# A gated FFN's input projection: whole-width split products replaced by seven half-size block products per pair of hidden tiles

## The chip, the cores and the metric

The kernel runs on one core of one Trainium2 chip. The metric is the device time of one launch in microseconds (us). The kernel before takes 932.84 us (median of three runs, 931.05 to 935.1). Engines: PE is TensorE (PEld its weight loads), DVE is VectorE, ACT is ScalarE, POOL is GpSimd, SP is the engine whose queue starts most DMAs.

## What is computed

One decoder layer on x (512 tokens, 1024 channels), float32: a combined input projection with three token mixers (a state-space scan, sparse attention, pooling), a gated merge, an output projection with residual, then the part that the change touches:

```python
h = h + merged @ w_out
hn = _rmsnorm(h, norm2_w)
a_part, b_part = jnp.split(hn @ w_ffn_in, 2, axis=-1)     # 1024 x (2 * 2816)
return h + (jax.nn.silu(a_part) * b_part) @ w_ffn_out      # 2816 x 1024
```

and a final RMSNorm over the channels.

## The kernel before

All matrix products are made in split precision: a float32 operand is split into a high part in the reduced format float32r (a cast on ACT, `ACT.copy(h, src)`) and a low part (`DVE.tensor_tensor(l, src, h, subtract)`). Three matmuls make one product term: high weight by high input, high weight by low input, low weight by high input (`product`, three `PE.matmul` for each 128-row slice k of the contraction).

- **Stages.** Input projection with the mixers; the branch projections; `w_out` (token-major, `token_major`); the norm of its result, tile of 128 tokens by tile (`residual`, `after_out`, which transposes the rows on PE into feature-major `hnh` and `hnl`); the FFN input; the FFN output (`token_major` again); final norm and stores.
- **FFN input.** 11 steps j. Each loads 256 gate columns (`ra`) and 256 value columns (`rb`) of `w_ffn_in`, 1 MB each, on SP's queue, into a ring of two raw buffers. For each of the 22 hidden tiles i of 128 columns it splits two weight slices of 128 x 1024 (tiles `wh`, `wl`, rings of three) and makes two products of 8 slices: 8 x 3 matmuls of 512 moving columns for the gate, as many for the value. They land in two PSUM banks `f`. Then `silu` on ACT, a product on DVE, and the split of the hidden tile into `hidh`, `hidl`.
- **First tiles.** The first three of these products are made in halves of 256 tokens (`for c in halves`), so that they can start before the norm of the last two token tiles is done; their weights (`early`, tiles `eh`, `el`) are split ahead, during `w_out`.
- **Order.** PE's order is the program's order (`manual_schedule`); small streams (norms, transposes) are put between the matmuls by `tick`. On the other engines a scheduler places the instructions when the program is built; each engine then runs its list strictly in order.
- **FFN output.** `token_major` walks the 22 hidden tiles; of each, 24 matmuls of 512 columns with the hidden tile as the weight side, and one split of a 128 x 1024 row block of `w_ffn_out`. The split hidden tiles are there since the stage before.

Of the kernel before, what the change touches and what calls it, by code (L numbers as in the profile page):

```python
# [8 lines left out]
F32 = mybir.dt.float32  # L9
# [4 lines left out]
P = 128  # L14
T = 512
# [80 lines left out]
def kernel(  # L96
# [91 lines left out]
    def nm(s):  # L188
        uid[0] += 1
        return f"{s}_{uid[0]}"  # L190
# [4 lines left out]
    def slot(tag, name, dtype=F32, shape=(P, T)):  # L195
        return spool.tile(list(shape), dtype, name=nm(name), tag=tag, bufs=SLOTS[tag])
# [4 lines left out]
    def pmm(name="mm"):  # L201
        return psum.tile([P, T], F32, name=nm(name), tag="mm")
# [7 lines left out]
    def tsl(t):  # L210
        return slice(t * P, (t + 1) * P)

    def load_cols(parts, nk):
        raw = wpool.tile([P, 2048], F32, name=nm("raw"), tag="raw", bufs=2)
        width = 2048 // nk
        rv = raw.rearrange("p (k n) -> p k n", k=nk)
        o = 0
        for ap, c0, n in parts:
            SP.dma_start(rv[:, :, o:o + n], ap[:, c0:c0 + n].rearrange("(k p) n -> p k n", p=P))
            o += n  # L220
        assert o <= width
        return rv
# [17 lines left out]
    def split(src, h, l):  # L240
        ACT.copy(h, src)
        DVE.tensor_tensor(l, src, h, op=OP.subtract)
# [51 lines left out]
    def to_feature_major(src, hs, ls, t, get):  # L294
        for g in range(2):
            ps = get("tr")
            for i in range(4):
                PE.transpose(ps[:, tsl(i)], src(4 * g + i), ident)
            pv = ps.rearrange("p (k t) -> p k t", k=4)
            split(pv, hs[g][:, :, tsl(t)], ls[g][:, :, tsl(t)])  # L300
            yield "now"
# [652 lines left out]
            st.live[0][1] = at + NLAG  # L954
        return st

    def token_major(w, nk, ah, al, tail, done, ahead=None):
        acc = {}
        for t in range(NT):
            for hf in range(2):  # L960
                acc[t, hf] = pmm("acc") if t < 2 else paux("acc")
        keep = []

        def term(t, k, wh, wl, hfs=(0, 1)):
            a, b = ah(k)[:, tsl(t)], al(k)[:, tsl(t)]
            for hf in hfs:
                cs = slice(hf * T, hf * T + T)
                PE.matmul(acc[t, hf], lhsT=a, rhs=wh[:, cs], start=(k == 0), stop=False)
                PE.matmul(acc[t, hf], lhsT=a, rhs=wl[:, cs], start=False, stop=False)
            for hf in hfs:  # L970
                cs = slice(hf * T, hf * T + T)
                PE.matmul(acc[t, hf], lhsT=b, rhs=wh[:, cs], start=False, stop=(k == nk - 1))
            tick()

        for k in range(nk):
            if k % 2 == 0:
                raw = wpool.tile([P, 2, D], F32, name=nm("raw"), tag="raw", bufs=2)
# [31 lines left out]
    fnrow = load_row(final_norm_w, "fnrow")  # L1009

    hnh = [slot("xn", "hnh", R32, (P, 4, T)) for _ in range(2)]
    hnl = [slot("xn", "hnl", R32, (P, 4, T)) for _ in range(2)]

    def residual(t, a0, a1, row, last):
        st = small([P, 2], "st2")
        ys = []
        for hf, a in ((0, a0), (1, a1)):
            if last and hf == 0:
                with tc.issue_after(stats[0]):
                    DVE.tensor_tensor(xr[t][hf], a, xr[t][hf], op=OP.add)  # L1020
            else:
                DVE.tensor_tensor(xr[t][hf], a, xr[t][hf], op=OP.add)
            ACT.activation(a, xr[t][hf], AF.Square, scale=RD, accum_out=st[:, hf:hf + 1])
            y = slot("m", "rows")
            (DVE if last or (row is fnrow and hf) else POOL).tensor_tensor(y, xr[t][hf], row[hf], op=OP.mult)
            ys.append(y)
        rs = rstd_of(st)
        for hf in range(2):
            if row is fnrow and hf == 1:
# [3 lines left out]
        return ys  # L1033

    def after_out(t, a0, a1):
# [5 lines left out]
    early, fraw = {}, []  # L1041

    def parted(src):
        hs, ls = [], []
        for g in range(2):
            tag = "yP" if len(early) < 2 else "A"
            h, l = slot(tag, "eh", R32), slot(tag, "el", R32)
            hv, lv = h.rearrange("p (k n) -> p k n", k=4), l.rearrange("p (k n) -> p k n", k=4)
            split(src[:, 4 * g:4 * g + 4, :], hv, lv)
            hs.append(hv)  # L1050
            ls.append(lv)
        return lambda k: hs[k // 4][:, k % 4, :], lambda k: ls[k // 4][:, k % 4, :]

    def early_weights():
        ra = load_cols([(wfi, 0, 256)], KD)
        rb = load_cols([(wfi, FH, 256)], KD)
        fraw.extend((ra, rb))
        for key, r in ((("a", 0), ra[:, :, tsl(0)]), (("b", 0), rb[:, :, tsl(0)]), (("a", 1), ra[:, :, tsl(1)])):
            early[key] = parted(r)
# [7 lines left out]
    def hh(k):  # L1067
        return hnh[k // 4][:, k % 4, :]

    def hl(k):  # L1070
        return hnl[k // 4][:, k % 4, :]

    hidh, hidl, hbig = [], [], []
    for j in range(NH // 2):
        if j:
            ra = load_cols([(wfi, 256 * j, 256)], KD)
            rb = load_cols([(wfi, FH + 256 * j, 256)], KD)
        else:
            ra, rb = fraw
            for key in early:  # L1080
                early[key] = (pmm("f"), *early[key])
            for c in halves:
                for ps, wh, wl in early.values():
                    product(ps, wh, wl, hh, hl, KD, c)
                for st in norms2[2:]:
                    need(st)
        for s in range(2):
            i = 2 * j + s
            pab = []
            for key, r in ((("a", i), ra), (("b", i), rb)):  # L1090
                if key in early:
                    pab.append(early[key][0])
                    continue
                wh, wl = split_w(r[:, :, tsl(s)], (P, KD, P))
                ps = pmm("f")
                product(ps, wh, wl, hh, hl, KD)
                pab.append(ps)
            pa, pb = pab
            sa = slot("th", "silu")
            ACT.activation(sa, pa, AF.Silu)  # L1100
            DVE.tensor_tensor(sa, sa, pb, op=OP.mult)
            if 14 <= i < 18:
                if i == 14:
                    hbig = [slot("yA", "hidb", R32, (P, 4, T)) for _ in range(2)]
                h, l = hbig[0][:, i - 14, :], hbig[1][:, i - 14, :]
            else:
                tag = "m" if i < 4 else "yP" if i < 8 else "A" if i < 14 else "T1" if i < 20 else "T2"
                h = slot(tag, "hidh", R32)
                l = slot(tag, "hidl", R32)
            split(sa, h, l)  # L1110
            hidh.append(h)
            hidl.append(l)

    of = out[0]

# [33 lines left out]
```

## Time and profile before

| | |
|---|---|
| median of three runs | 932.84 us |
| the profiled execution | 933.53 us, of which 931.8 us is the span from its first to its last instruction |
| PE, PEld | 906.9 us (97%), 751.2 us (81%) of the span |
| DVE, ACT, POOL | 489.2 us (52%), 359.3 us (39%), 96.4 us (10%) |
| granted TensorE clock | 0.998 |
| HBM | 91 GB/s over the span |

PE's busy time counts overlapping matmuls: a row's duration is longer than the distance to the next one's start. What a matmul costs in a dense run is the distance of two starts. "[3.88 <-PE f]" behind a row means that the engine stood idle for 3.88 us before it and that a PE instruction on f ended this. The scheduler leaves lists in order, so an instruction that waits holds all behind it on its engine.

### The profile page before, as it was taken

To read this page: it belongs to the slowest core of one execution; us is meant where nothing else is said; L and a number is where in the kernel's file an instruction comes from. 1 tells how busy PE (TensorE), PEld (TensorE's weight loads), DVE (VectorE), ACT (ScalarE), POOL (GpSimd) and SP (SyncE) were. 2 spreads that over 40 slices of the span, in tenths; PEclk is the share of its full clock that TensorE was granted. 3 is DMA by queue.
4 is the path that set the end of the run, shared out by engine and by line. 5 is a ranking of instruction groups with operands and counts; after the bars stand their busy time and mean duration, and the time that the engine had idled before them with its cause. 6 is when DMAs were issued, how large, how long until landed. Compare 5 with 4: busy or idle time off the path is not lost.

```text
span 931.8 us, 11002 instructions
## 1 busy us (share of the span) xinstructions
PE 906.9 (97%) x4401; PEld 751.2 (81%) x4401; DVE 489.2 (52%) x792; ACT 359.3 (39%) x618; POOL 96.4 (10%) x96
## 2 busy tenths in 40 slices
PE   6999899999999999999999999999999999999997
PEld 4877678888888877778888889888888888888885
DVE  6487999955654576658343355233333333322226
ACT  5446433355564344545322256222232232212114
POOL 2061000001100133332000021000000000000001
PEclk9999999999999999999999999999999999999999
DMA  7132112232221311215223241222222332332212
GB/s 239 46 113 77 59 46 91 76 106 83 74 70 58 101 46 57 91 57 181 91 92 135 90 136 46 90 91 91 91 91 92 111 114 91 95 117 105 91 46 90
DMA packets 70964, 85.42 MB, mean 92 GB/s; under 512 B 4025, under 2 KB 61953, under 8 KB 70914
## 3 DMA queue, kind: packets, MB, share of 16 engines
q1 hardware_dynamic: 69234, 82.38, 27.3%
q10 hardware_dynamic: 1680, 2.36, 0.8%
q8 instruction: 34, 0.56, 0.2%
q14 instruction: 16, 0.13, 0.0%
HBM read 82.63 MB, written 2.10 MB: 91 GB/s over the span
## 4 chain that ended last, share of the span: by engine, by line
PE 85%; DVE 9%; issue 2%; ACT 2%; POOL 1%; DMA 0%; SPq 0%; POOLq 0%; ACTq 0%; DVEq 0%
PE mm L90 26%; PE f L90 26%; PE acc L90 17%; PE up L90 8%; DVE work L90 2%; DVE wl L90 2%; DVE top L90 2%; PE yatt L90 1%; PE yd L90 1%; PE ptr L90 1%; PE logit L90 1%; POOL win L90 1%; PE yo L90 1%; DVE qT L90 1%; PE state L90 1%
## 5 line engine op out<-in xcount | busy, mean ns | idle before, releaser
L90 DVE TENSOR_TENSOR wl<-raw,wh 128x1024 fp32r<-128x1024 f32 (+1 forms) x150 | 183.5, 1224 | 228.1 <-ACT wh L90 222.8
L90 ACT CAST wh<-raw 128x1024 fp32r<-128x1024 f32 (+1 forms) x152 | 152.7, 1005 | 378.9 <-PE f L90 155.6
L90 PE MATMUL mm<-xnh,wh 128*128 128x512 f32 (+1 forms) x480 | 193.9, 404 | 0.2 <-ACT xnh L90 0.2
L90 PE MATMUL mm<-xnl,wh 128*128 128x512 f32 (+1 forms) x480 | 183.5, 382 | 1.0 <-DVE xnl L90 1.0
L90 PE MATMUL mm<-xnh,wl 128*128 128x512 f32 (+1 forms) x480 | 183.7, 383 | 0.0
L90 PE MATMUL f<-hnh,wh 128*128 128x512 f32 x328 | 127.6, 389 | 0.0
L90 PE MATMUL f<-hnl,wh 128*128 128x512 f32 x328 | 127.6, 389 | 0.0
L90 PE MATMUL f<-hnh,wl 128*128 128x512 f32 x328 | 127.6, 389 | 0.0
L90 PEld LDWEIGHTS mm<-xnh,wl 128*128 128x128 f32 x480 | 91.1, 190 | 17.9
L90 PEld LDWEIGHTS mm<-xnl,wh 128*128 128x128 f32 x480 | 91.5, 191 | 16.1 <-DVE xnl L90 1.5
L90 PEld LDWEIGHTS mm<-xnh,wh 128*128 128x128 f32 x480 | 91.7, 191 | 15.5 <-issue 1.6
L90 PEld LDWEIGHTS f<-hnh,wl 128*128 128x128 f32 x328 | 61.6, 188 | 12.9
L90 PEld LDWEIGHTS f<-hnl,wh 128*128 128x128 f32 x328 | 61.6, 188 | 12.8
L90 PEld LDWEIGHTS f<-hnh,wh 128*128 128x128 f32 x328 | 61.6, 188 | 12.6
L90 DVE TENSOR_TENSOR silu<-silu,f 128x512 f32<-128x512 f32 x22 | 15.1, 688 | 78.2 <-PE f L90 78.2
L90 PE MATMUL acc<-wh,hidh 128*128 128x512 f32 x144 | 56.0, 389 | 0.0
L90 PE MATMUL acc<-wl,hidh 128*128 128x512 f32 x144 | 56.0, 389 | 0.0
L90 PE MATMUL acc<-wh,hidl 128*128 128x512 f32 x144 | 44.8, 389 | 0.0
L90 POOL TENSOR_TENSOR rows<-xr,fnrow 128x512 f32<-128x512 f32 x3 | 3.9, 1292 | 353.1 <-issue 347.5
L90 POOL TENSOR_TENSOR xbc<-xbc,tap 128x509 f32<-128x509 f32 x12 | 14.0, 1164 | 194.8 <-DVE xbc L90 167.1
L90 PEld LDWEIGHTS acc<-wl,hidh 128*128 128x128 f32 x144 | 27.0, 188 | 5.6
L90 PEld LDWEIGHTS acc<-wh,hidl 128*128 128x128 f32 x144 | 27.0, 188 | 5.6
(250 smaller groups left out, 1322.9 us busy)
## 6 DMA issues: line engine op xcount, KB each, us to landing
raw<-in_w_in_dram SPq DMA_DIRECT2D x26, 1024.0 KB, 5.0
raw<-in_w_ffn_in_dram SPq DMA_DIRECT2D x22, 1024.0 KB, 4.9
raw<-in_w_ffn_out_dram SPq DMA_DIRECT2D x11, 1024.0 KB, 5.0
raw<-in_w_up_ssd_dram SPq DMA_DIRECT2D x4, 1024.0 KB, 4.7
raw<-in_w_out_dram SPq DMA_DIRECT2D x4, 1024.0 KB, 5.0
xb<-in_x_dram SPq DMA_DIRECT2D x4, 512.0 KB, 4.3
raw<-in_w_in_dram SPq DMA_DIRECT2D x4, 512.0 KB, 5.9
raw<-in_w_up_pool_dram SPq DMA_DIRECT2D x2, 1024.0 KB, 4.9
```

What stands on the lines that cost most here:

```text
L90: return fn(*args, **kw)
```

## The change

The 512 tokens are cut into two halves of 256 and the 1024 contraction rows into two halves of 512; gate and value columns are taken as the two block rows of one matrix. For each of 11 units u (256 gate and 256 value columns) seven products p replace eight block products. Each has 4 slices of 128, two blocks c of 128 output rows, three matmuls of 256 columns: 24 x 7 = 168 matmuls for a unit, where 96 of 512 columns stood. The input blocks are B11, B21 (first 256 tokens, two channel halves), the differences T1 to T4, and B22. The weight sums and differences are made by DVE on the raw weights, in place (`combine_w`).

Bank r1 of a unit collects products 1, 6, 7 and 4 one after the other. Between them ACT copies its state out (`keep`, into `p1`, `u2`, `u3`), since two results need the state after 1, after 6 and after 7. Products 2 and 5, 3 have banks of their own. DVE adds the copies (`added`), ACT applies silu, DVE multiplies. Split hidden tiles are no longer made in this stage: the hidden tile stays whole (`hid`) and is split in the FFN output (`hidden_part`). The residual rows are written to a DRAM scratch and read back for the FFN output. The first three units begin with their products 1 and 2; then come 5, 6, 7, 4, 3. All others run 1, 5, 6, 2, 7, 4, 3. Weights of the product at place n + 2 are split when place n is issued (`prepare`).

```diff
 def after_out(t, a0, a1):
     hn = residual(t, a0, a1, n2row, False)
-    yield
-    yield from to_feature_major(lambda k: hn[k // 4][:, tsl(k % 4)], hnh, hnl, t, pmm if t < 2 else paux)
+    for hf in range(2):
+        SP.dma_start(hrows[t][hf], xr[t][hf])
+    yield
+    for g in range(2):
+        ...
+        if t < 2:
+            split(pv, tl[:, 0, :, cs], tl[:, 1, :, cs])
+        for j in range(2):
+            ACT.copy(w[j][:, :, cs], pv[:, 2 * j:2 * j + 2, :])
+        yield "now"
+def combine_x(name):
+    ...
+    for j in range(2):
+        if x is not None:
+            DVE.tensor_tensor(o[j], x[j], y[j], op=OP.subtract)
+        split(o[j], h[j], l[j])
+def combine_w(u, p):
+    if p == 5:
+        for j in range(2):
+            DVE.tensor_tensor(first_sum[u][j], raws[u][1][:, 2 * j:2 * j + 2, :], raws[u][1][:, 4 + 2 * j:6 + 2 * j, :], op=OP.add)
+    elif p == 6:
+        DVE.tensor_tensor(quarter(u, 1, 0), quarter(u, 0, 0), quarter(u, 1, 0), op=sub)
+        for j in range(2):
+            a = raws[u][0][:, 2 * j:2 * j + 2, :]
+            DVE.tensor_tensor(a, first_sum[u][j], a, op=sub)
+    elif p == 3:
+        DVE.tensor_tensor(quarter(u, 0, 1), quarter(u, 0, 1), quarter(u, 0, 0), op=sub)
+def weights(u, p):
+    h = wpool.tile([P, 4, HW], R32, name=nm("wh"), tag="wh")
+    l = wpool.tile([P, 4, HW], R32, name=nm("wl"), tag="wl")
+    ...
+def early_weights():
+    ...
+    for u in range(2):
+        for p in (1, 2):
+            h, l = (pieces("A" if p == 1 else "yP", "early", R32) for _ in range(2))
+            for j in range(2):
+                split(quarter(u, *WHERE[p])[:, 2 * j:2 * j + 2, :], h[j], l[j])
+def multiply(u, p):
+    r, first = {1: (1, True), 6: (1, False), 7: (1, False), 4: (1, False), 2: (2, True), 5: (3, True), 3: (3, False)}[p]
+    ...
+    for c in range(2):
+        o = ps[:, c * HW:c * HW + HW]
+        for k in range(4):
+            a, b = xh[k // 2][:, k % 2, :], xl[k // 2][:, k % 2, :]
+            PE.matmul(o, lhsT=wh(k)[:, tsl(c)], rhs=a, ...)
+            PE.matmul(o, lhsT=wh(k)[:, tsl(c)], rhs=b, ...)
+            PE.matmul(o, lhsT=wl(k)[:, tsl(c)], rhs=a, ...)
+            tick()
+def keep(u, name):
+    snap[u, name] = slot("th", name)
+    ACT.copy(snap[u, name], res[u, 1])
+def added(u, r, name):
+    c = slot("A", "cs")
+    DVE.tensor_tensor(c, res[u, r], snap[u, name], op=OP.add)
+    return c
+def collect(u, p):
+    if p == 1:
+        keep(u, "p1")
+    elif p == 2:
+        a0 = added(u, 2, "p1")          # then silu of two halves on ACT
+    elif p == 6:
+        keep(u, "u2")
+    elif p == 7:
+        keep(u, "u3")
+        gate_[u] = added(u, 3, "u3")
+    elif p == 4:
+        ...                              # hid (first tokens) *= r1
+    elif p == 3:
+        a1 = added(u, 3, "u2")          # silu, then hid (last tokens) = a1 * gate_
+plan = [(u, p) for u in range(LEADERS) for p in (1, 2)]
+for u in range(NU):
+    plan += [(u, p) for p in ((5, 6, 7, 4, 3) if u < LEADERS else (1, 5, 6, 2, 7, 4, 3))]
+for n, (u, p) in enumerate(plan):
+    ...
+    if n in XSUMS:
+        combine_x(XSUMS[n])
+    prepare(n + 2)
+    multiply(u, p)
+    collect(u, p)
-token_major(w_ffn_out[0], NH, lambda k: hidh[k], lambda k: hidl[k], 3, after_ffn)
+token_major(w_ffn_out[0], NH, lambda k: hidden_part(k, 0), lambda k: hidden_part(k, 1), 3, after_ffn, tag="xn")
```

**Where the lists change.** ACT, one unit from the fourth on (here the sixth; `raw_5625` holds its value weights, `raw_5623` its gate weights, `raw_5857` the gate weights of the next unit; `r_1063` is its bank r1). Products in PE's order: 2 (`wh_5992`), 7 (`wh_6021`), 4 (`wh_6051`), 3 (`wh_6087`), then the next unit's 1 (`wh_6123`) and 5 (`wh_6157`).

```order
L90 CAST wh_6051<-raw_5625 128x1024
L90 COPY u_1070_6049<-r_1063_5965 128x512
L90 CAST wh_6087<-raw_5623 128x1024
L90 ACTIVATE hid_6083<-cs_6081 128x256
L90 ACTIVATE hid_6085<-cs_6081 128x256
L90 CAST wh_6123<-raw_5857 128x1024
L90 COPY u_1081_6119<-r_1063_5965 128x512
L90 CAST wh_6157<-S_1085_6127 128x512
L90 CAST wh_6157<-S_1086_6128 128x512
L90 CAST wh_6195<-raw_5857 128x1024
```

The same place before:

```order
L90 CAST wh_5704<-raw_5700 128x1024
L90 CAST hidh_5631<-silu_5628 128x512
L90 CAST wh_5733<-raw_5702 128x1024
L90 ACTIVATE silu_5693<-f_5639 128x512
L90 CAST wh_5769<-raw_5700 128x1024
```

What moved: where ACT had casts and one silu on a bank that nothing adds to any more, it now has three copies of a bank that PE goes on adding to. The copy after product 7 (`u_1081`) stands behind the cast of the next unit's first weights (`wh_6123`), whose ring place product 7 itself gives back.

ACT in the first three units (here the first: products 7 `wh_4974`, 4 `wh_5013`, 3 `wh_5049`, then product 5 of the second unit, `wh_5089`):

```order
L90 CAST wh_5013<-raw_4490 128x1024
L90 CAST T_945_5004<-whole_4639 128x512
L90 CAST wh_5049<-raw_4488 128x1024
L90 COPY u_950_5042<-r_895_4714 128x512
L90 CAST wh_5089<-S_956_5057 128x512
L90 COPY u_958_5085<-r_895_4714 128x512
L90 CAST wh_5089<-S_957_5058 128x512
L90 CAST wh_5124<-raw_4492 128x1024
```

What moved: product 7 now follows product 6 at once on the same bank, so two copies stand between successive products, each behind the cast of a later product's weights: a cast of 128x1024 before `u_950`, one of 128x512 before `u_958`.

ACT at the start of the FFN output (`wh_7370`, `wh_7402`, `wh_7436` are the first three row blocks of `w_ffn_out`, `cs_7335` the last silu of the last unit, `hidh_7374` the high part of hidden tile 0):

```order
L90 CAST wh_7370<-raw_7368 128x1024
L90 COPY u_1222_7281<-r_1210_7162 128x512
L90 CAST wh_7402<-raw_7368 128x1024
L90 CAST wh_7436<-raw_7434 128x1024
L90 ACTIVATE cs_7335<-cs_7335 128x512
L90 CAST hidh_7374<-hid_4800 128x512
L90 CAST hidh_7406<-hid_4802 128x512
```

What moved: the splits of the hidden tiles, which stood in the stage before, now begin behind the last unit's silu.

## Rows read from the trace of the kernel before

**Rows 1.** The page: busy time of the engines, and the shares of the chain of work that ended last, by engine.

```profile
PE 906.9 (97%) x4401; PEld 751.2 (81%) x4401; DVE 489.2 (52%) x792; ACT 359.3 (39%) x618; POOL 96.4 (10%) x96
PE 85%; DVE 9%; issue 2%; ACT 2%; POOL 1%; DMA 0%; SPq 0%; POOLq 0%; ACTq 0%; DVEq 0%
```

**Rows 2.** Busy time by stretch: the stages before `w_out`, and the FFN input. Columns: PE, PEld, DVE, ACT, POOL busy, granted clock, DMA share, GB/s.

```profile
0.00:518.00 518.00, 499.50 (x2522) 411.13 (x2523) 342.68 (x621) 232.19 (x436) 81.83 (x85) 1.00 0.29 90
563.20:805.50 242.30, 242.30 (x1145) 203.75 (x1144) 84.94 (x93) 73.80 (x99) 2.09 (x2) 1.00 0.29 94
```

**Rows 3.** The tile `f` (results of the FFN input): duration of one in ns (least, median, most), first and last start in us. One of the three kinds of 512-column matmuls (all three have 328), then one of the three kinds of 256-column ones of the early halves (48 each), with its weight load.

```profile
L90 PE MATMUL f<-hnh,wh x328: 389/389/396, 582.4 to 804.8; 128*128 128x512 f32 x164
L90 PEld LDWEIGHTS f<-hnh,eh x48: 187/192/192, 563.0 to 582.0; 128*128 128x128 f32 x48
L90 PE MATMUL f<-hnh,eh x48: 278/283/368, 563.2 to 582.1; 128*128 128x256 f32 x48
```

**Rows 4.** Timeline of PE around the last undisturbed run of 256-column matmuls: its first, and the last of it with the first 512-column one. 57 of them lie between 575.61 and 582.44.

```profile
575.61 0.28 PE L90 MATMUL f<-hnh,eh 128*128 128x256 f32 x1
...
582.32 0.28 PE L90 MATMUL f<-hnh,el 128*128 128x256 f32 x1
582.44 0.40 PE L90 MATMUL f<-hnh,wh 128*128 128x512 f32 x1
```

**Rows 5.** Timeline of ACT in the FFN input: a weight cast and the instruction behind it, twice.

```profile
642.32 1.06 ACT L90 CAST wh<-raw 128x1024 fp32r<-128x1024 f32 x1 [3.88 <-PE f L90]
643.30 0.62 ACT L90 CAST hidh<-silu 128x512 fp32r<-128x512 f32 x1
647.76 1.05 ACT L90 CAST wh<-raw 128x1024 fp32r<-128x1024 f32 x1 [3.84 <-PE f L90]
648.72 0.58 ACT L90 ACTIVATE silu<-f 128x512 f32<-128x512 f32 x1
```

**Rows 6.** Timelines of PE and DVE at a border of two products: the last matmul of one that reads its `wh` (one more, on `wl`, stands behind it), and the first of the next; and DVE behind it.

```profile
641.85 0.39 PE L90 MATMUL f<-hnl,wh 128*128 128x512 f32 x1
...
642.31 0.39 PE L90 MATMUL f<-hnh,wh 128*128 128x512 f32 x1
...
642.58 0.69 DVE L90 TENSOR_TENSOR silu<-silu,f 128x512 f32<-128x512 f32 x1 [3.38 <-PE f L90]
643.41 1.23 DVE L90 TENSOR_TENSOR wl<-raw,wh 128x1024 fp32r<-128x1024 f32 x1
644.56 0.68 DVE L90 TENSOR_TENSOR hidl<-silu,hidh 128x512 fp32r<-128x512 f32 x1
```

**Rows 7.** Timelines of ACT and PE in the first stage, where PE waits for ACT: the releasing instruction, the two matmuls behind the wait, the next one.

```profile
80.54 0.60 ACT L90 ACTIVATE relu<-score 128x512 f32<-128x512 f32 x1
81.19 0.74 PE L90 MATMUL score<-ki,qi 128*128 128x512 f32 x2 [0.40 <-ACT relu L90]
81.77 0.40 PE L90 MATMUL mm<-xnh,wh 128*128 128x512 f32 x1
```

**Rows 8.** Groups of DVE and of ACT between 563.2 and 805.6 us: count, busy us, mean ns of one, idle before.

```profile
L90 DVE TENSOR_TENSOR wl<-raw,wh 128x1024 fp32r<-128x1024 f32 x43 | 53.7, 1249 | 77.6 <-ACT wh L90 76.1
L90 DVE TENSOR_TENSOR silu<-silu,f 128x512 f32<-128x512 f32 x21 | 14.4, 688 | 74.9 <-PE f L90 74.9
L90 ACT CAST wh<-raw 128x1024 fp32r<-128x1024 f32 x44 | 46.3, 1052 | 161.1 <-PE f L90 155.6 <-issue 3.9 <-DMA raw<-in_w_ffn_in_dram 1.6
```

**Rows 9.** Loads of `w_ffn_in`: the page's row of DMA issues (count, KB, median us from issue to landing), and one pair on SP's queue.

```profile
raw<-in_w_ffn_in_dram SPq DMA_DIRECT2D x22, 1024.0 KB, 4.9
655.55 5.80 SPq L219 DMA_DIRECT2D raw<-in_w_ffn_in_dram  x2
```

**Rows 10.** Timelines in `w_out` and behind it: ACT and DVE splitting the early weights, the last weight block of `w_out`, PE where it needs this; then DVE beside a POOL multiplication, the last norm rows on ACT, and the chain's transposes of the last token tile.

```profile
541.57 2.19 ACT L90 CAST eh<-raw 128x512 fp32r<-128x512 f32 x4 [0.72 <-DMA raw<-in_w_ffn_in_dram]
545.23 1.05 ACT L90 CAST wh<-raw 128x1024 fp32r<-128x1024 f32 x1 [1.48 <-PE acc L90]
542.23 2.50 DVE L90 TENSOR_TENSOR el<-raw,eh 128x512 fp32r<-128x512 f32 x4
546.32 1.22 DVE L90 TENSOR_TENSOR wl<-raw,wh 128x1024 fp32r<-128x1024 f32 x1 [1.60 <-ACT wh L90]
547.98 0.39 PE L90 MATMUL acc<-wl,mgh 128*128 128x512 f32 x1
...
565.10 2.25 DVE L90 TENSOR_TENSOR wl<-raw,wh 128x1024 fp32r<-128x1024 f32 x1 [0.27 <-ACT wh L90]
564.97 1.30 POOL L90 TENSOR_TENSOR rows<-xr,n2row 128x512 f32<-128x512 f32 x1 [0.98 <-DVE xr L90]
567.65 0.20 ACT L90 ACTIVATE rs<-ms 128x1 f32<-128x1 f32 x1 [1.02 <-DVE ms L90]
568.23 1.33 ACT L90 ACTIVATE rows<-rows,rs 128x512 f32<-128x512 f32 x2
569.67 0.44 PE tr L90 x4
```

**Rows 11.** Timelines of PE and ACT where the FFN output begins.

```profile
805.28 0.39 PE L90 MATMUL f<-hnh,wl 128*128 128x512 f32 x1
805.51 0.39 PE L90 MATMUL acc<-wh,hidh 128*128 128x512 f32 x1
...
805.52 1.06 ACT L90 CAST wh<-raw 128x1024 fp32r<-128x1024 f32 x1 [3.88 <-issue]
```

More of the change, by code (lines that the diff above doesn't have):

```diff
@@ L976, in token_major @@
             if k % 2 == 0:
-                raw = wpool.tile([P, 2, D], F32, name=nm("raw"), tag="raw", bufs=2)
+                raw = (slot(tag, "raw", F32, (P, 2, D)) if tag else
+                       wpool.tile([P, 2, D], F32, name=nm("raw"), tag="raw", bufs=2))
                 SP.dma_start(raw, w[k * P:(k + 2) * P, :].rearrange("(k p) n -> p k n", p=P))
@@ L1024, in residual @@
             y = slot("m", "rows")
-            (DVE if last or (row is fnrow and hf) else POOL).tensor_tensor(y, xr[t][hf], row[hf], op=OP.mult)
+            (DVE if last or (row is not n2row and hf) else POOL).tensor_tensor(y, xr[t][hf], row[hf], op=OP.mult)
             ys.append(y)
@@ L1028, in residual @@
         for hf in range(2):
-            if row is fnrow and hf == 1:
+            if row is not n2row and hf == 1:
                 DVE.tensor_scalar(ys[hf], ys[hf], rs, None, OP.mult)
@@ L1033, in residual, with k4, pieces @@
         return ys
+    dram = ctx.enter_context(tc.tile_pool(name="rows", bufs=1, space=bass.MemoryType.DRAM))
+    hrows = [[dram.tile([P, T], F32, name=f"hrows_{t}_{hf}", tag=f"hrows_{t}_{hf}") for hf in range(2)] for t in range(NT)]
+    HW = T // 2
+    NU = NH // 2
+    G = dict(skip_group_check=True)
+    def k4(ap):
+        return ap.rearrange("p (k t) -> p k t", k=4)
+    def pieces(tag, name, dtype=F32):
+        return [slot(tag, name, dtype, (P, 2, HW)) for _ in range(2)]
+    blocks, whole = {}, {}
@@ L1035, in after_out, with block @@
+    def block(name):
+        if name not in blocks:
+            if name in ("B11", "B21", "T1", "B22"):
+                tl = slot("xn" if name in ("B11", "B21") else "yA", name, R32, (P, 2, 4, HW))
+                blocks[name] = [[tl[:, i, 2 * j:2 * j + 2, :] for j in range(2)] for i in range(2)]
+                blocks[name].append(tl)
+            else:
+                blocks[name] = [pieces("xbc", name, R32) for _ in range(2)]
+        return blocks[name]
     def after_out(t, a0, a1):
@@ L1054, in early_weights @@
-    def early_weights():
[L1055 to L1059, printed above, removed]
+        cs = tsl(t % 2)
+        for g in range(2):
+            ps = (pmm if t < 2 else paux)("tr")
+            for i in range(4):
+                PE.transpose(ps[:, tsl(i)], hn[g][:, tsl(i)], ident)
+            pv = k4(ps)
+            if t < 2:
+                tl = block(("B11", "B21")[g])[2]
+                split(pv, tl[:, 0, :, cs], tl[:, 1, :, cs])
+            w = whole.setdefault((g, t // 2), [])
+            if not w:
+                w.extend(pieces("A" if t < 2 else "T2", "whole"))
+            for j in range(2):
+                ACT.copy(w[j][:, :, cs], pv[:, 2 * j:2 * j + 2, :])
+            yield "now"
@@ new lines, in combine_x @@
+    def combine_x(name):
+        b11, b21, b12, b22 = (whole[g, t] for t in range(2) for g in range(2))
+        o, x, y = {"T1": (b11, b12, b11), "T2": (b11, b22, b11), "T3": (b12, b22, b12), "T4": (b21, b21, b11),
+                   "B22": (b22, None, None)}[name]
+        h, l = block(name)[:2]
+        for j in range(2):
+            if x is not None:
+                DVE.tensor_tensor(o[j], x[j], y[j], op=OP.subtract)
+            split(o[j], h[j], l[j])
+    wfi = w_ffn_in[0]
+    raws, ahead_raw, first_sum, parts, res, snap = {}, {}, {}, {}, {}, {}
@@ new lines, with load_raw, load_unit, quarter @@
+    gate_, hid = {}, {}
+    def load_raw(u, ab, tag):
+        rv = (wpool.tile([P, KD, 256], F32, name=nm("raw"), tag="raw", bufs=2) if tag == "raw"
+              else slot(tag, "raw", F32, (P, KD, 256)))
+        c0 = ab * FH + 256 * u
+        SP.dma_start(rv, wfi[:, c0:c0 + 256].rearrange("(k p) n -> p k n", p=P))
+        return rv
+    def load_unit(u):
+        if 2 <= u < NU:
+            raws[u] = [load_raw(u, ab, "xn" if u % 2 else "raw") for ab in range(2)]
+    def quarter(u, i, j):
+        return raws[u][i][:, 4 * j:4 * j + 4, :]
@@ new lines @@
+    WHERE = {1: (0, 0), 2: (0, 1), 3: (0, 1), 4: (1, 1), 6: (0, 0), 7: (1, 0)}
+    RHS = {1: "B11", 2: "B21", 3: "B22", 4: "T4", 5: "T1", 6: "T2", 7: "T3"}
+    def weights(u, p):
+        if (u, p) in parts:
+            return
+        h = wpool.tile([P, 4, HW], R32, name=nm("wh"), tag="wh")
+        l = wpool.tile([P, 4, HW], R32, name=nm("wl"), tag="wl")
+        if p == 5:
+            for j in range(2):
+                split(first_sum[u][j], h[:, 2 * j:2 * j + 2, :], l[:, 2 * j:2 * j + 2, :])
+        elif u in ahead_raw and p in (1, 2):
+            i, j = WHERE[p]
+            split(ahead_raw[u][:, 4 * j:4 * j + 4, :], h, l)
+        else:
+            split(quarter(u, *WHERE[p]), h, l)
+        parts[u, p] = (lambda k: h[:, k, :]), (lambda k: l[:, k, :])
@@ new lines, in multiply @@
+    def multiply(u, p):
+        r, first = {1: (1, True), 6: (1, False), 7: (1, False), 4: (1, False), 2: (2, True), 5: (3, True), 3: (3, False)}[p]
+        if first:
+            res[u, r] = (pmm if r == 1 else paux)(f"r{r}")
+        ps = res[u, r]
+        wh, wl = parts.pop((u, p))
+        xh, xl = block(RHS[p])[:2]
+        for c in range(2):
+            o = ps[:, c * HW:c * HW + HW]
+            for k in range(4):
+                a, b = xh[k // 2][:, k % 2, :], xl[k // 2][:, k % 2, :]
+                PE.matmul(o, lhsT=wh(k)[:, tsl(c)], rhs=a, start=first and k == 0 and c == 0, stop=False, **G)
+                PE.matmul(o, lhsT=wh(k)[:, tsl(c)], rhs=b, start=False, stop=False, **G)
+                PE.matmul(o, lhsT=wl(k)[:, tsl(c)], rhs=a, start=False, stop=k == 3 and c == 1, **G)
+                tick()
@@ new lines, in keep @@
+    def keep(u, name):
[10 more added lines that the diff above has]
+            a0 = added(u, 2, "p1")
+            for c in range(2):
+                i = 2 * u + c
+                hid[i] = slot("T2" if i < 4 or 8 <= i < 12 else "T1" if i < 8 else "yP" if i < 20 else "A", "hid")
+                ACT.activation(hid[i][:, :HW], a0[:, c * HW:c * HW + HW], AF.Silu)
+        elif p == 6:
[4 more added lines that the diff above has]
+        elif p == 4:
+            for c in range(2):
+                h = hid[2 * u + c][:, :HW]
+                DVE.tensor_tensor(h, h, res[u, 1][:, c * HW:c * HW + HW], op=OP.mult)
+        elif p == 3:
+            a1 = added(u, 3, "u2")
+            ACT.activation(a1, a1, AF.Silu)
+            for c in range(2):
+                cs = slice(c * HW, c * HW + HW)
+                DVE.tensor_tensor(hid[2 * u + c][:, HW:], a1[:, cs], gate_[u][:, cs], op=OP.mult)
@@ L1065 @@
         need(st)
[L1067 to L1112, printed above, removed]
@@ new lines @@
+    prepare(0)
+    prepare(1)
+    for n, (u, p) in enumerate(plan):
+        if n == 3:
+            for st in norms2[2:]:
+                need(st)
+        if n in XSUMS:
[3 more added lines that the diff above has]
+        collect(u, p)
+    fnrow = load_row(final_norm_w, "fnrow")
+    xr = [[slot("xbc", "xr") for _ in range(2)] for _ in range(NT)]
+    for t in range(NT):
+        for hf in range(2):
+            SP.dma_start(xr[t][hf], hrows[t][hf])
+    hidden = {}
@@ L1114, with hidden_part @@
+    def hidden_part(k, part):
+        if k not in hidden:
+            h, l = slot("A", "hidh", R32), slot("A", "hidl", R32)
+            split(hid[k], h, l)
+            hidden[k] = h, l
+        return hidden[k][part]
     of = out[0]
```

36 lines of the change are left out of this document (21 added, 15 removed).

## The prediction, made before the changed kernel ran

> **What bounds the kernel now.** I read the page's busy times and its chain first: PE is busy 97% of the span and makes 85% of the chain [rows 1]. That alone says little about one stage, so the busy times by stretch come next: between 563.2 and 805.5 us PE is busy for all of 242.3 us, DVE for 84.9, ACT for 73.8 [rows 2]. The FFN input is matmuls back to back, and what it costs is their number times their distance.
>
> The distances come from starts, not from durations. From 582.44 [rows 4] to 805.51 [rows 11] stand 3 x 328 = 984 matmuls of 512 columns [rows 3]: 223.07 / 984 = 226.7 ns each, although a row lasts 389. The early halves show the other size: 57 matmuls of 256 columns between 575.61 and 582.44 [rows 4], 6.83 / 57 = 119.8 ns. Half the columns cost 53% of the time.
>
> **The matmuls: -18.9 us.** Before: 984 x 226.7 ns + 3 x 48 x 119.8 ns = 223.1 + 17.2 = 240.3 us. After: 11 units x 168 x 119.8 ns = 221.4 us. An eighth of the products goes, and 6% of a matmul comes back each time it is cut in half; 7.9% of the stage is left. The transposes of the norm stay as they are.
>
> A weight load lasts 192 ns [rows 3], longer than the distance of 120, and is hidden. The Trainium skill (TensorE: Matmul & The Clock Gate, Measured speedup vs the span model) says that a weight load overlaps running matmuls only where it uses another row group, which no load here does; by that rule each of the 1,848 matmuls would lie open, and the sum would be the last rival's. The trace does not agree.
>
> **The copies out of r1: +25.1 us.** Product 7 adds to the bank that ACT must have copied as it stood after product 6, and product 4 to the one as it stood after 7. In units from the fourth on, product 2 (24 x 0.12 = 2.9 us) lies between 6 and 7, and product 5 between 1 and 6; these two copies are covered: cast, copy and latencies take 1.85 us as worked out below. Nothing lies between 7 and 4. There ACT's list has the cast for the next unit's product 1 ahead of the copy, and that cast waits for product 7 too, because the ring of three gives it product 7's place. I count from the slot in which PE would start product 4:
> - The last matmul of product 7 that reads `wh` starts two slots earlier and lasts 0.28 [rows 3]; in the same situation ACT started 0.08 behind the end of such a matmul: 641.85 + 0.39 [rows 6] against 642.32 [rows 5]. So the cast starts at -0.24 + 0.28 + 0.08 = 0.12.
> - A cast of 128 x 1024 holds ACT for 0.97 (642.32 to 643.30, 647.76 to 648.72 [rows 5]): 1.09.
> - The copy of a 128 x 512 bank takes the 0.58 of the silu on such a bank [rows 5]: 1.67.
> - PE starts 0.05 behind ACT (80.54 + 0.60 to 81.19), and its first matmul behind a wait takes 0.13 longer than two distances leave (81.77 - 81.19 - 2 x 0.227) [rows 7]: **1.85 us**.
>
> Eight units pay this once. The first three have 6, 7, 4 in direct succession. Each pays 1.85 at product 7; at product 4 the first two pay 1.43, since the cast in front has 512 columns there (0.55, [rows 10]), the third 1.85. Together 12 x 1.85 + 2 x 1.43 = 25.1 us. Bounds: 1.00 for each of the 14, were the copy first in line (the product's last matmul ends 0.16 into the slot, 0.08, then 0.58 and 0.18), and 2.2 if ACT's two instructions take their whole row durations (1.05, 0.59) and the latencies double. I take the value from ACT's own rows, because nothing else is in that list.
>
> **DVE, hidden.** A unit needs eight instructions of 1024 columns at 1.15 (643.41 to 644.56 [rows 6]), nine of 512 at 0.61 (2.50 less an overlap of 0.07, over four [rows 10]) and four of 256, between 0.3 and 0.61: 9.2 + 5.5 + 1.5 = 16.2 us; with whole row durations (1.25, 0.69 [rows 8]) 18. PE's unit is 168 x 0.1198 + 1.85 = 22.0. A ring place comes free three products ahead of its next use; cast and low part take 2.3 us of the two products left, 5.8, so DVE may be late by some 3 us. The cover is PE's time alone; there are 4 us of it in a unit. ACT needs ten of 22. Loads: two of 1 MB per unit in 5.8 us [rows 9]; they start when the unit two before has split its product 3 and are wanted by DVE some 7 us later. DVE would wait for them with its other work behind it, which its 3 us cover.
>
> **The start: +1.6 us.** (a) The early weights grow from six to eight splits of 512 columns, all ahead of `w_out`'s last weight block in the lists. ACT casts from 541.57 at 0.55 each [rows 10], so until 545.97; then the block's cast to 546.94, its low part on DVE to 548.15. PE wants it at 547.98 [rows 10]: 0.2 us, and 0.2 for the restart. (b) The rows of the last token tile reach PE just in time now (568.23 + 1.33 against 569.67 [rows 10]), about 6.4 us into the stage; the new place of their transposes is as deep. ACT gets eight more copies of 256 columns ahead of them (0.32 to 0.55 each, no row has this shape; I take the low end, since a shorter copy cannot be dearer), 2.6 us; 0.4 comes back since a copy of 0.58 stands where a cast of 0.97 stood, and 1.0 is idle there today [rows 10]. That leaves 1.2. Bounds of the start 0 to 5, the upper one if DVE's instructions beside POOL's take 2.25 in place of 1.25, as one did [rows 10, 8]. The x differences follow under the second rival.
>
> **The end of the stage: +2.9 us.** Today the FFN output follows without a gap (805.28, 805.51 [rows 11]), since its hidden tiles lie ready. Now the first one's split stands in ACT's list behind a cast that waits for the last product's ring place and behind the last silu: 0.12 + 0.97 + 0.55 + 0.60 (the split's cast) + 0.18 = 2.4 us until the first matmul. Its low part comes 0.5 us later than the fifth matmul wants it (DVE: low part of a weight block, two 256-column products, then this). Bounds 1 and 4. Later hidden tiles are hidden: 1.1 + 0.6 us of ACT and 1.25 + 0.69 of DVE in 24 x 0.227 = 5.4 us of PE. Residual rows to DRAM and back: hidden, the reload is wanted a hundred us later.
>
> **The sum.** -18.9 + 25.1 + 1.6 + 2.9 = +10.7 us. Against the profiled execution's own 933.53 us that is 944.2; the median of the runs shown lies 0.7 lower, so I give **944**. With the waits a quarter us shorter or longer (14 x 0.25 = 3.5) and the bounds of start and end: 938 to 951. A measurement of this kernel tells about 0.5% (4.7 us) from no change.
>
> **Rivals.**
> - **Only the copy is paid, not slower** (7%). If the cast in front of each copy found its ring place free before product 7 ends, the 14 waits would shrink to about 1.00: -18.9 + 14.0 + 4.5 = -0.4 us, 933. Below (18.9 - 4.5) / 14 = 1.03 us a wait the change is no slower; below 0.7 it would be faster by over 0.5%. [...]
> - **DVE late in the first units** (11%). From product 1 of the first unit to its product 3 DVE has some 8 instructions of 1024 and 29 of 512 columns (norm, weight sums, T1 to T4, B22): 27 us, with whole row durations and 0.1 of waiting at each 34, in eleven products and two waits of PE, 34.9. Past that point PE pays. With a fifth more than the 34, from waits on ACT's splits and on POOL as in [rows 10], it pays 6: 950.
> - **Late loads** (2%). At twice the 5.8 us [rows 9] the loads miss DVE by 4 us and PE by 1 to 2 in each unit: 960. Loads at a third of the DMA time [rows 2] speak against it.
> - **Weight loads come into the open** (2%). With 192 ns per matmul in place of 120 the stage grows by 1,848 x 0.072 = 133 us: 1,077. Against it: the 57 matmuls [rows 4] are the same shape on the same kind of operands. Nor does the clock look endangered: it is 1.00 in the first stretch, where PE idles for 18 us in all [rows 2].
>
> That the products are made as said is plain from the list: 1,848 matmuls of 256 columns on the banks r1 to r3.
>
> **Chances.** Forecast 78%, rivals 7, 11, 2, 2. Faster by over 0.5%: 2 (what of the first rival lies below 0.7 us a wait). Within: 9 (the rest of it, and the forecast's lowest end). Slower: 89. The range takes the forecast's bounds and most of the second rival: 937 to 953.
>
> **What would show it.** In the changed profile: r matmuls at 120 ns; in each unit from the fourth one idle time of PE of 1.7 to 1.9 us that ends with ACT's copy, with a cast of 1024 columns right before that copy; six such waits in the first three units; 22 us a unit; a gap of 2 to 3 us where the FFN output begins; DVE busy for 16 to 18 us a unit. It is wrong if PE waits for DVE's low parts instead, if the copies find the bank in time, or if 256-column matmuls stand wider apart than 125 ns, where this term alone grows by 10 us.

## The result: 1.3% slower, and the profile after

The changed kernel takes 945.67 us (median of 4 runs, 943.78 to 945.93) against 933.16 for the kernel before in the same comparison: a ratio of 1.013, 95% interval 1.0104 to 1.0156. The prediction was 944, slower, from 937 to 953. The profiled execution took 945.64 us, its span 943.9, which is 12.1 more than the 931.8 before.

The page of the changed kernel, the two rows that answer to [rows 1]:

```profile
PE 896.4 (95%) x5121; PEld 774.6 (82%) x5121; DVE 612.4 (65%) x972; ACT 419.9 (44%) x729; POOL 95.6 (10%) x96
...
PE 29%; ACT 2%; issue 2%; DVE 1%
```

The waits of PE from 500 us on (what it waited for: us in total, times, longest):

```profile
PE r L90 <- ACT u L90: 20.8, 14, 1.6
PE acc L90 <- ACT hidh L90: 2.1, 1, 2.1
PE acc L90 <- DVE wl L90: 0.3, 1, 0.3
PE tr L90 <- ACT rows L90: 0.3, 1, 0.3
PE acc L90 <- DVE hidl L90: 0.3, 1, 0.3
```

PE is busy for 10.5 us less than before and the kernel is longer all the same: 14 waits for a copy `u` out of r1 have come in, the number the prediction counted. (The chain reaches back over a third of the span here, so its shares can't be set beside those of before.) DVE's busy time has grown by 123 us, and from 500 us on PE waits for it for no more than 0.3 us at any place. By stage: `w_out`, the FFN input (as the second row of [rows 2]) and what follows it (columns as in [rows 2]):

```profile
517.00:564.90 47.90, 47.56 (x217) 39.03 (x216) 23.99 (x34) 22.86 (x46) 8.65 (x7) 1.00 0.36 126
564.90:813.30 248.40, 227.27 (x1865) 224.19 (x1863) 191.28 (x248) 121.24 (x183) 1.88 (x2) 1.00 0.33 110
813.30:940.00 126.70, 121.92 (x530) 100.07 (x528) 53.60 (x70) 42.76 (x68) 3.89 (x3) 0.99 0.20 71
```

The stages begin at their first matmuls and end one matmul slot behind their last: before at 517.83, 563.24 and 805.51, with the end of the span at 931.83; now at 518.83, 564.91 and 813.31, with the end at 943.93. The FFN input takes 248.4 us for 242.3 (+6.1). `w_out` takes 46.1 for 45.4 (+0.7), what follows the FFN input 130.6 for 126.3 (+4.3), and `w_out` begins 1.0 us later, ahead of everything the change touches. Together 12.1.

In the steady units the chain of waits repeats every 21.965 us (start, us, what), and the timelines of PE and ACT at the same place show a wait from inside, as [rows 5, 7] show its parts before:

```profile
652.13 1.04 ACT wh L90
653.17 0.49 ACT u L90
...
653.71 18.87 PE r L90 x156
...
675.68 18.87 PE r L90 x156
```

```profile
652.13 1.04 ACT L90 CAST wh<-raw 128x1024 fp32r<-128x1024 f32 x1 [1.21 <-issue]
653.08 0.58 ACT L90 COPY u<-r 128x512 f32<-128x512 f32 x1
...
651.89 0.28 PE L90 MATMUL r<-T,wl 128*128 128x256 f32 x1
653.71 0.51 PE L90 MATMUL r<-T,wh 128*128 128x256 f32 x2 [1.55 <-ACT u L90]
```

Product 7's last matmul starts at 651.89, the next would follow at 652.01. ACT starts its cast at 652.13, the copy at 653.08, and PE goes on at 653.71. The profile names no releaser for that cast ("issue"); that it waits for product 7 is read from the time, since the last matmul that reads `wh` starts at 651.77 and its row ends at 652.05, 0.08 before the cast, the distance foreseen. The idle time in brackets (1.55) is shorter than the loss, because it counts from the end of a row of 0.28 us and not from the slot 0.12 behind its start, and leaves out the slower restart. The loss is read from starts: 21.965 - 168 x 0.1198 = 1.84 us a unit.

### The profile page after: what moved, and what is told of

It reads as the page before. It is cut to its first block, busy times and chain, and to the rows that moved or that the text cites. A ratio compares the mean times of both kernels' runs of the same rounds, so it can differ in the third digit from the quotient of the medians.

```text
span 943.9 us, 12826 instructions
## 1 busy us (share of the span) xinstructions
PE 896.4 (95%) x5121; PEld 774.6 (82%) x5121; DVE 612.4 (65%) x972; ACT 419.9 (44%) x729; POOL 95.6 (10%) x96
## 5 line engine op out<-in xcount | busy, mean ns | idle before, releaser
L90 DVE TENSOR_TENSOR wl<-raw,wh 128x1024 fp32r<-128x1024 f32 (+1 forms) x171 | 207.6, 1214 | 122.7 <-ACT wh L90 118.3
L90 PE MATMUL r<-T,wh 128*128 128x256 f32 x704 | 129.5, 285 | 20.8 <-ACT u L90 20.8
L90 PEld LDWEIGHTS r<-T,wh 128*128 128x128 f32 x704 | 109.5, 192 | 23.6 <-ACT u L90 23.6
L90 PEld LDWEIGHTS mm<-xnl,wh 128*128 128x128 f32 x480 | 92.2, 192 | 16.2 <-DVE xnl L90 1.6
L90 PE MATMUL r<-T,wl 128*128 128x256 f32 x352 | 99.5, 283 | 0.0
L90 PE MATMUL r<-B,wh 128*128 128x256 f32 x464 | 84.4, 283 | 0.0
L90 PEld LDWEIGHTS r<-B,wh 128*128 128x128 f32 x464 | 72.4, 192 | 0.0
L90 PEld LDWEIGHTS r<-T,wl 128*128 128x128 f32 x352 | 67.5, 192 | 0.0
L90 PE MATMUL r<-B,wl 128*128 128x256 f32 x232 | 65.7, 283 | 0.0
L90 PEld LDWEIGHTS r<-B,wl 128*128 128x128 f32 x232 | 44.5, 192 | 0.0
L90 PEld LDWEIGHTS acc<-wh,hidh 128*128 128x128 f32 x176 | 33.4, 190 | 9.3 <-ACT hidh L90 2.3
```

Of the source, the lines that this page charges most:

```text
L90: return fn(*args, **kw)
```

## Where the FFN output begins

Timelines of PE, ACT and DVE there, which answer to [rows 11], and the granted clock (column 6 behind the stretch, after the five engines) in stretches of 2 us:

```profile
813.19 0.28 PE L90 MATMUL r<-B,wl 128*128 128x256 f32 x1
815.53 0.50 PE L90 MATMUL acc<-wh,hidh 128*128 128x512 f32 x1 [2.06 <-ACT hidh L90]
817.02 1.22 PE L90 MATMUL acc<-wh,hidl 128*128 128x512 f32 x2 [0.30 <-DVE hidl L90]
818.04 0.63 PE L90 MATMUL acc<-wh,hidh 128*128 128x512 f32 x1
...
820.45 0.40 PE L90 MATMUL acc<-wh,hidh 128*128 128x512 f32 x1
...
813.39 1.04 ACT L90 CAST wh<-raw 128x1024 fp32r<-128x1024 f32 x1 [1.78 <-PE r L90]
814.34 0.63 ACT L90 ACTIVATE cs<-cs 128x512 f32<-128x512 f32 x1
814.88 2.69 ACT L90 CAST hidh<-hid 128x512 fp32r<-128x512 f32 x5
...
816.28 3.09 DVE L90 TENSOR_TENSOR hidl<-hid,hidh 128x512 fp32r<-128x512 f32 x5
```

```profile
814.00:816.00 2.00, 0.47 (x2) 0.43 (x3) 1.73 (x4) 2.00 (x5) 0.00 (x0) 1.00 0.83 260
816.00:818.00 2.00, 1.70 (x6) 1.07 (x5) 2.00 (x5) 1.56 (x3) 0.00 (x0) 0.71 0.61 250
818.00:820.00 2.00, 2.00 (x6) 1.57 (x5) 1.38 (x3) 0.00 (x0) 0.00 (x0) 0.50 0.00 0
```

The gap is there with its parts in the order foreseen: cast, silu, the first split, and a second short wait for the low part. What was not foreseen stands behind it. From 817.0 to 820.4 the matmuls lie 0.43 us apart in place of 0.23, at a granted clock that falls to 0.50, the lower of the two levels.

## The experiments

The theory: the block products lose because PE waits for ACT's copy of r1 wherever no other product lies between two that add into r1, and ACT has a weight cast ahead of that copy. The rivals: only the copy matters; VectorE's sums set the pace; halving the matmuls costs more than the rows said. The kernel before was measured again beside the runs, at 933.41 us beside the first four and 933.81 beside the last three, for 933.16 beside the changed kernel; so a difference from the changed kernel's 945.67 is good to about 0.7 us. Where it matters, the stages of the profiled executions are compared as well.

**Another product between 7 and 4, in the later units.**

```diff
-        plan += [(u, p) for p in (... (1, 5, 6, 2, 7, 4, 3))]
...
+            if u == LEADERS:
+                plan.append((u, 1))
+            plan += [(u, 5), (u, 6), (u, 2), (u, 7)] + [(u + 1, 1)] * (u + 1 < NU) + [(u, 4), (u, 3)]
```

> From the fourth unit on, the next unit's product 1 is multiplied between this unit's products 7 and 4, with nothing else changed. Theory (TensorE waits at product 4 for ScalarE's copy of r1, behind a cast of 1024): 2.9 us of matmuls now stand between the end of product 7 and product 4, the cast and the copy take 1.6, so the waits of units 3 to 10 go: 8 x 1.85 = 14.8 us less than the changed kernel's 945.7, about 931; the unit falls from 21.97 us to 20.1, and six waits are left in the first three units. Rival 'only the copy is paid': 8 x 1.00 = 8.0 less, about 937.7. Rival 'VectorE is the bound in the units': the period stays near 22 us, about 945.

Measured: 932.22 us (ratio to the kernel before 0.9985, 0.9976 to 0.9995), 13.5 less than the changed kernel. The waits of PE from 560 us on, and then the chain of waits from 650 to 760 us:

```profile
PE r L90 <- ACT u L90: 10.0, 7, 1.6
```

```profile
649.92 110.16 PE r L90 x918
```

In the steady units PE never stops: 110.16 / 918 = 120.0 ns a matmul. Seven waits are left, one more than expected: the last unit has no next product 1 to put between, so seven waits went, not eight, 7 x 1.84 = 12.9 us, and the FFN input takes 235.8 us, 12.6 less than in the changed kernel. My count was off by one; the price of a wait was not. Neither rival holds here: at 1.00 a wait 7 us would have come, and VectorE, with 16.6 us of work a unit, keeps up with units of 20.1.

**The copy ahead of the cast.**

```diff
-        ACT.copy(snap[u, name], res[u, 1])
+        last_keep[0] = ACT.copy(snap[u, name], res[u, 1]).ins
...
-        weights(u, p)
...
+            with tc.issue_after(last_keep[0]):
+                weights(u, p)
```

> TensorE's order is untouched; on ScalarE the weight casts stand behind the copy of r1 that they stood ahead of. Theory: the copy then starts at the end of the product, and each of the 14 waits falls to about 1.00 us, so 12 x 0.85 + 2 x 0.43 = 11.1 us less than the changed kernel, about 934.6, the unit 21.1 us. Rival 'the cast costs nothing, it is the accumulator's turnaround': nothing moves, about 945.7. If the later casts make the weights late, part of the gain returns as waits for wh or wl.

Measured: 935.2 us (1.0015, 1.0005 to 1.0025), 10.5 less than the changed kernel. The waits of PE from 560 us on, and then the timelines of ACT and PE at product 4 of a steady unit, and at product 4 of the last unit:

```profile
PE r L90 <- ACT u L90: 10.3, 14, 1.5
```

```profile
668.16 0.59 ACT L90 COPY u<-r 128x512 f32<-128x512 f32 x1 [1.28 <-PE r L90]
668.64 1.05 ACT L90 CAST wh<-raw 128x1024 fp32r<-128x1024 f32 x1
...
668.80 0.51 PE L90 MATMUL r<-T,wh 128*128 128x256 f32 x2 [0.68 <-ACT u L90]
```

```profile
794.65 1.04 ACT L90 CAST wh<-raw 128x1024 fp32r<-128x1024 f32 x1 [1.21 <-issue]
795.60 0.58 ACT L90 COPY u<-r 128x512 f32<-128x512 f32 x1
...
796.23 0.51 PE L90 MATMUL r<-T,wh 128*128 128x256 f32 x2 [1.55 <-ACT u L90]
```

All 14 waits are still there. Thirteen have fallen to 0.68 us of idle time, 0.97 by starts (the steady unit takes 21.09 us), where 1.00 was foreseen. The last unit's wait at product 4 has not moved: the cast ahead of its copy makes the first weights of `w_ffn_out`, which the edit doesn't reach, and it still takes 1.55. One wait that keeps its cast keeps its length, thirteen that lose it shrink. PE's order is untouched, so the cast ahead of the copy is shown to cost about 10 of the 25 us (the FFN input falls from 248.4 to 238.4 us, though the transposes of the last token tile come 0.5 later), and the rival by which the cast costs nothing falls. Putting the copy first is the first rival's world, and its 933 is near.

**The kernel before in halves.**

```diff
-                product(ps, wh, wl, hh, hl, KD)
+                for c in halves:
+                    product(ps, wh, wl, hh, hl, KD, c)
```

> The kernel before, with the FFN input's products multiplied in two halves of 256 tokens: 2112 matmuls of 256 columns for 984 of 512 and 144 of 256. Theory: a half costs 119.8 ns against 226.7 for the whole, so 2112 x 119.8 = 253.0 us for 240.3, 12.7 more than the kernel before, about 945.9; seven eighths of that less, 221.4, is what the block products cost. Rival 'the weight loads come into the open at 256 columns': each load 192 ns, 2112 x 192 = 405.5, 165 more. Rival 'halves cost nothing': 933.2.

Measured: 947.48 us (1.0144, 1.0127 to 1.016), 14.1 over the kernel before. Tile `f`, weight load and matmul (duration in ns: least, median, most; first and last start):

```profile
L90 PEld LDWEIGHTS f<-hnh,wh x656: 192/192/192, 583.7 to 819.5; 128*128 128x128 f32 x164
L90 PE MATMUL f<-hnh,wh x656: 283/283/283, 583.8 to 819.6; 128*128 128x256 f32 x164
```

The FFN input takes 255.3 us (564.67 to 819.94), 13.0 more than before, for 12.7 expected. It begins 1.4 us later than before: 0.6 are there already at the gap at 113 us, and 0.8 come behind it, where the clock fell in this execution (below). So halving costs 13 us, an eighth less products gives 32 back (253.0 to 221.4), and a weight load of 192 ns is hidden at a distance of 121 (255.3 us for 2112 matmuls and the transposes of the norm). Both together are the -18.9 of the sum.

**The first hidden tiles split early.**

```diff
...
         prepare(n + 2)
+        if n == len(plan) - 3:
+            for k in range(3):
+                hidden_part(k, 0)
         multiply(u, p)
```

> The changed kernel, with the high and low parts of the first three hidden tiles made ahead of the last three products. Theory: the FFN output's first matmul no longer waits 2.1 us for the first high part and 0.3 for the low part, 2.9 less with what the front of the stage lost; and if the low clock behind that gap (matmuls 0.43 us apart for 3.4 us) comes of the gap, it goes too, 1.7 more: about 941.1. Rival 'the clock falls there anyway': about 942.8 with the 0.43 us rows still there. Rival 'the first weights of the stage end last': the gap stays near 2 us with another tile's name, about 945.

Measured: 939.89 us (1.0068, 1.0054 to 1.0082), 5.8 less than the changed kernel. The timeline of PE where the last product ends, and then the stretch behind it with the clock; last, ACT and PE at product 4 of the last unit:

```profile
811.85 0.28 PE L90 MATMUL r<-B,wl 128*128 128x256 f32 x1
811.97 0.40 PE L90 MATMUL acc<-wh,hidh 128*128 128x512 f32 x1
```

```profile
812.00:814.00 2.00, 2.00 (x11) 1.67 (x10) 1.56 (x2) 1.95 (x3) 0.00 (x0) 1.00 0.56 159
```

```profile
805.49 0.57 ACT L90 COPY u<-r 128x512 f32<-128x512 f32 x1
...
806.11 0.51 PE L90 MATMUL r<-T,wh 128*128 128x256 f32 x2 [0.84 <-ACT u L90]
```

Gap and low clock are both gone: from 811.97 to the end of the span are 126.2 us, as before the change (126.3) and 4.4 less than in the changed kernel. The other 1.3 us of the gain lie ahead of that border. 0.7 of them lie before the FFN input, where this execution kept its clock (below). The remaining 0.7 are the last unit's wait at product 4, 0.84 for 1.55: with the new splits in ACT's list the weight cast has moved behind the copy, a second effect of this edit, which the expectation doesn't name.

**Another product between everywhere, alone and with the early splits.**

```diff
-    for u in range(NU):
-        plan += [(u, p) for p in (... (1, 5, 6, 2, 7, 4, 3))]
+    lead = [(0, 5), (0, 6), (1, 5), (0, 7), (1, 6), (0, 4), (1, 7), (0, 3), (1, 4), (1, 3),
+            (2, 5), (2, 6), (3, 1), (2, 7), (3, 5), (2, 4), (2, 3), (3, 6), (3, 2), (3, 7), (4, 1), (3, 4), (3, 3)]
+    plan += lead
+    for u in range(LEADERS + 1, NU):
+        plan += [(u, 5), (u, 6), (u, 2), (u, 7)] + [(u + 1, 1)] * (u + 1 < NU) + [(u, 4), (u, 3)]
```

> The changed kernel with another product between any two that add into one r1, in the first units too (products of units 0 and 1 alternate, then those of 2 with the first of 3). Theory: all 14 waits go, 25.1 us less than the changed kernel's 945.7, about 920.6; against the run with the later units alone (932.2) 10 to 11.6 less. Rival 'VectorE is late in the first units', where it makes the token sums beside the weight sums: waits for wl or for the parts of T1 to T4 appear in the first 60 us of the stage, and only some of that gain comes: 924 to 930.

> The same order, and the parts of the first three hidden tiles made ahead of the last three products. Theory: both gains add, 25.1 for the waits and the 5.8 that the early parts measured alone: about 914.8, some 18 under the kernel before: the 18.9 of the matmuls, less the start of the stage. Rival 'the two gains overlap' (with the waits gone VectorE and ScalarE are later at the end of the stage): the gap at the FFN output comes back, about 918 to 920.

Measured: 921.74 us (0.9872, 0.9855 to 0.9888) alone, and 917.86 us (0.9827, 0.9812 to 0.9842) with the early splits. The waits of PE in the first from 500 us on; its clock behind the gap at the FFN output, which it still has; then the waits in the second:

```profile
PE acc L90 <- ACT hidh L90: 2.1, 1, 2.1
PE r L90 <- ACT u L90: 1.5, 1, 1.5
...
PE r L90 <- DVE wl L90: 0.2, 1, 0.2
```

```profile
792.00:794.00 2.00, 1.70 (x7) 1.10 (x7) 2.00 (x5) 1.79 (x4) 0.00 (x0) 1.00 0.71 289
```

```profile
PE r L90 <- ACT u L90: 0.8, 1, 0.8
```

Thirteen waits go; the last unit's stays, as in the first of these runs, so that "all 14" was off by one again. The FFN input takes 226.6 us for 248.4, 21.8 less, where thirteen waits were priced at 22.9. The time falls by 23.9; what lies outside the stage is mostly clock, which the profiled execution kept at both places where the changed kernel's had lost it (below). VectorE is late in the first units by 0.2 us, so that rival is nearly nothing even with PE at full pace there.

The early splits bring 3.9 more, not 5.8. Between the two profiled executions it is 3.5: 2.9 for the gap and 0.7 for the last unit's wait (1.55 to 0.84), less small differences. The 5.8 held 1.5 of low clock behind the gap and 0.7 from before the FFN input as well, and the order without the splits kept its clock there in its profiled execution; for its other executions this is not shown. The second kernel is 1.7% faster than the kernel before: the gain of the seven products was there, and its waits hid it. 917.9 is 3 us over my 914.8: 1.1 of that are the last unit's wait, which was to go (783.06 - 781.94 from start to start); the other 1.9 fit those parts of the 5.8 that had come already, but no run separates them.

**More work for VectorE.**

```diff
             split(quarter(u, *WHERE[p]), h, l)
+            if p in (2, 6, 7):
+                DVE.tensor_tensor(l, quarter(u, *WHERE[p]), h, op=OP.subtract)
```

> The changed kernel, with the low parts of the weights of products 2, 6 and 7 subtracted twice on VectorE: 128x1024 elements, 1.23 us each, 3.7 more a unit and 34 such operations in all or a few fewer, some 40 us of VectorE. Theory (VectorE's 16.2 of 22 us a unit are hidden, with some 4 free): the time stays within 2 us of 945.7, with small waits in the first three units at most. Rival 'VectorE sets the pace of the units': each microsecond shows, 30 to 40 more, 975 to 985.

Measured: 945.79 us (1.0126, 1.0111 to 1.0141), where the changed kernel has 945.67. Two units of 22 us, first here and then in the changed kernel (DVE is the third of the busy times):

```profile
650.00:694.00 44.00, 40.90 (x339) 40.50 (x338) 39.04 (x49) 20.36 (x28) 0.00 (x0) 1.00 0.29 97
```

```profile
650.00:694.00 44.00, 40.91 (x339) 40.50 (x338) 33.11 (x43) 20.23 (x29) 0.00 (x0) 1.00 0.30 97
```

VectorE does 3.0 us more a unit (1.0 for each repeat, under the 1.23 I had put), is busy 89% of the time, and in these units nothing is later. Its 16.6 us a unit in the changed kernel are hidden, with at least 3 to spare. In the first unit one wait has grown by 0.5 us (ACT and PE at its product 7):

```profile
590.26 0.61 ACT L90 CAST T<-whole 128x512 fp32r<-128x512 f32 x1
591.41 0.76 PE L90 MATMUL r<-T,wh 128*128 128x256 f32 x2 [2.08 <-ACT u L90]
```

PE does not wait for VectorE there: in ACT's list a cast of 512 columns now stands between the weight cast and the copy, which the changed kernel's list does not have at that place. With the fall of the clock behind that wait (below) the FFN input takes 250.5 us in this execution, 2.1 more, and the median is still the same. How much cover the first units have is not measured: from 585 to 607 us VectorE is busy for 21.7 of 22 us in the changed kernel already.

## Why the prediction was right, point by point

- **The matmuls, -18.9.** 120.0 ns a matmul where PE doesn't stop, 119.8 foreseen: 1,848 of them are 221.8 us, so -18.5.
- **The copies out of r1, +25.1.** The mechanism, the number of waits and their places are as put. From start to start, twelve cost 1.82 to 1.84 us (1.85 foreseen) and the two behind a cast of 512 columns 1.36 and 1.40 (1.43): some 24.7. The interleaved order took thirteen of them away, and the changed order on ACT cut thirteen to 0.97.
- **VectorE, ACT and the loads, hidden.** 16.6 us a unit for 16.2 (at most 18); PE waits for one low part in `w_out` and for one hidden tile's, 0.3 each. The run with more work shows the cover.
- **The start, +1.6.** `w_out` grew by 0.7 for 0.4. The transposes of the last token tile came 0.3 to 0.5 us late for 1.2. The copies of 256 columns take 0.31 us each (5.0 us of ACT for 16), as the 0.32 that I had put without a row (that a shorter copy cannot be dearer gave only the upper bound, 0.55); it is the delay of PE behind them that I had put too high.
- **The end of the stage, +2.9: the step that was mis-sized.** The gap and the wait for the low part together are 2.9 us, as put, by the run that kept its clock there (129.1 us from the last product to the end, against 126.2 with the early splits). In the changed kernel the clock then fell as well, and 1.5 us more went: 130.6, which is 4.3 over the 126.3 before. The prediction asked about the clock only for the idle time of the first stage, and didn't ask what this gap would do to it. The 1.00 that it read there was that of one execution: behind an idle time in that same stage the clock fell in two of the nine traces.
- **Outside the sum, +1.0.** `w_out` begins that much later, because the clock fell at 112 to 120 us in the changed kernel's profiled execution: from the gap at 113 us to `w_out` are 405.4 us here and 404.3 before. The seven traces that kept the clock there, six of them with the changed stage, have 404.3 to 404.5.

The sum was 10.7. The profile has 12.1, of which 2.5 are those two falls of the clock; without them it would be 9.6. So the nearness of 944 to 945.67 is in part luck: the terms foreseen came out 1.1 too high, and what was not foreseen added 2.5. (The bounds named add up to 937 to 952, not 938 to 951; nothing hangs on it.) The rivals fell each by its row: ACT's list has the cast ahead of the copy at 652.13, PE waits for VectorE nowhere in the first units, DVE waits 1.0 us in all for loads, and the weight loads stay at 192 ns under matmuls 120 apart. The rule on such loads that the prediction quotes from the Trainium skill (TensorE: Matmul & The Clock Gate) stands there in the section The mechanism, not in the one named, and that section also lets a load be pulled ahead when it goes to the background weight buffer. So the last rival does not follow from that page as a whole.

## What to carry to other kernels

A cheaper set of matmuls that adds several products into one bank, with a copy of the bank between them, is paid for by the copy's latency at each place where nothing else lies between; count those places in TensorE's order, and price each from the engine that copies, with whatever stands ahead of the copy in its list. What helped here is another product in between, which cost nothing in thirteen places, and, where that can't be had, the copy first in its engine's list (0.97 us in place of 1.84). At the end of a stage look which operand the next one wants first, and make it before the last products.

## What the runs showed of the hardware that was not expected

The clock behind a gap of PE differs from execution to execution. PE sits idle for 1.86 to 1.89 us at 111 to 114 us in every kernel here; behind it the granted clock fell in two of nine traces. In the changed kernel (first) it fell, in the kernel before (second) not:

```profile
112.00:116.00 4.00, 2.57 (x7) 2.08 (x8) 3.65 (x11) 0.87 (x4) 0.00 (x0) 0.71 0.00 0
116.00:120.00 4.00, 4.00 (x20) 3.35 (x18) 3.40 (x13) 1.35 (x4) 0.00 (x0) 0.86 0.00 0
```

```profile
112.00:116.00 4.00, 2.44 (x12) 2.09 (x13) 3.83 (x13) 1.68 (x5) 0.00 (x0) 1.00 0.00 0
```

Behind the 2.06 us at the FFN output it fell in four of the five traces that have this gap, for about 3.4 us at 0.50 and a loss of 1.0 to 1.5 (130.1 to 130.6 us from the last product to the end, against 129.1). Behind the fourteen waits of 1.1 to 1.6 us it fell in none of the changed kernel. In the run with more work for VectorE one of those waits had grown to 2.08 us, and the clock fell behind that one. What decides in which execution it falls stays open; no run was made for it. The changed kernel's own executions show the size: three with a mean granted clock of 0.994 took 945.6 to 945.9 us, the one with 0.998 took 943.8. Differences of 1 to 2 us between two single executions can be this alone.
